# A fifth tile by quarters in both feed-forwards, and the second one's weight sums made in DRAM by accumulating DMAs

## The chip, the cores and the metric

One Trainium2 chip; the kernel runs on one of its cores. The metric is the device time of one execution in microseconds (us), the median of several runs. The engines are named as the profile names them: PE is TensorE (matmuls), with PEld its weight loads; DVE is VectorE, ACT is ScalarE, POOL is GpSimd, and SP is SyncE, which here only issues DMAs. Each engine works through its own queue in order and waits on semaphores for the others.

## The reference

One decoder layer for 512 tokens of width 1024, all in float32:

```python
# x: (1, 512, 1024); D_FF = 2816
x = x + 0.5 * rms_norm(swiglu_ffn(rms_norm(x, pre[0]), ffn1_w_in, ffn1_w_out), post[0])
x = x + rms_norm(token_mixer(rms_norm(x, pre[1]), w_mix_in, ..., w_mix_out), post[1])
x = x + 0.5 * rms_norm(swiglu_ffn(rms_norm(x, pre[2]), ffn2_w_in, ffn2_w_out), post[2])

def swiglu_ffn(x, w_in, w_out):
    gate, up = jnp.split(x @ w_in, 2, axis=-1)
    return (jax.nn.silu(gate) * up) @ w_out
```

The token mixer (two recurrences over chunks, HGRN2 and mLSTM, between two projections) isn't touched by the change.

## The kernel before

The three parts of the layer follow one another: first feed-forward ("f1", about the first 340 us), mixer (to about 600 us), second feed-forward ("f2", to the end).

**Exact products.** Every float32 operand is split into a high part, rounded by ACT (a cast, line 273 for weights, 812 for activations), and a low part, the rest, by DVE (lines 275 and 813). A product takes three matmuls: high by high, high by low, low by high.

**Seven products for eight.** Both feed-forwards multiply by Winograd's form of Strassen's method: two-by-two blocks are multiplied with seven products instead of eight, at the price of sums of blocks before and after. In the first half of a feed-forward (`ffn_in`) the products are called p1 to p7, and each tile `t` of the 11 tiles of 256 hidden columns goes through all seven, 24 matmuls each. Four blocks of raw weights (a, b, c, d) are loaded for a tile, and they are added to one another in place (line 289), by POOL for the early tiles (t under 3) and by DVE for the later ones.

**The output stage** (`ffn_out`) multiplies the gated activations, in 11 tiles k2 of 256 hidden rows, by the output weights. It makes the 1024 output columns in two halves of 512; `OUT` gives the order of the tiles in each half. A tile is done plainly (`plain`, line 893: 48 matmuls of 256 columns) or, if it is in `QUARTERED` for this half, by quarters (`quartered`, line 901: 42 matmuls in seven products). A tile by quarters needs of the activations three quarters (`h_quarters`) and four sums (`h_sums`, then `s_tile`), which are kept if the tile is quartered in both halves; and of the weights three quarters (one item, cut to 768 columns) and four sums, a second item without a load of its own. The sums of weight quarters are made in place in the raw buffer:

```python
for out, a, c in ((1, 1, 0), (0, 0, 2), (2, 1, 2), (3, 2, 3)):
    self.nc.vector.tensor_tensor(b[out], b[a], b[c], op=ALU.add)   # line 306
```

The common part of all quartered tiles of a half is gathered in four PSUM banks M, turned into T at the end (`common`) and added to the output banks C (`add`). The last four tiles (`LAST`) of the second half are held together and done token chunk by token chunk, so that each chunk's norm and residual can follow while PE does the next.

**Buffers.** Four split weights (`w`) are made ahead of PE. Raw weights lie in two rings, `raw` with 3 buffers and `raw2` with 5. Activation tiles of the output stage have a ring `s` of 3; some are put into the dead transposed input instead (`PLACES`, `LATER`, through `x_place`). The quarters of tiles 3 and 7 lie in the ring `raw` ("once"). Tiles 9 and 10 are used in both halves and keep their split (`AGAIN`).

**Order.** The code is traced into one program; a scheduler of the framework then orders each engine's queue by readiness in its own plan, with the order of the code as priority, and assigns buffers and semaphores. Where the code says `behind(...)`, an instruction is queued after another one. `Item` stands for one split weight, `Load` for one DMA; `weights` works out after which item each load is due. Loads go through SP's queue.

Of the kernel before, what the change touches and what calls it, by code (L numbers as in the profile page):

```python
# [8 lines left out]
F32 = mybir.dt.float32  # L9
F32R = mybir.dt.float32r  # L10
AF = mybir.ActivationFunctionType
ALU = mybir.AluOpType
PSUM = bass.MemoryType.PSUM

P = 128
T = 512
D = 1024
# [5 lines left out]
RAW, WBUF, PAD, LATE, NEXT, FRONT, STEP = 3, 4, 128, 112, 64, 96, 16  # L23
# [55 lines left out]

QUARTERED = [(2, 3, 4, 6, 7, 8), (2, 4, 6, 8)]
OUT = [list(range(PAIRS)), [9, 2, 4, 10, 6, 8, 0, 1, 3, 5, 7]]
LAST = 4
PLACES, LATER = {2: 1, 4: 2, 6: 0, 8: 3}, {0: (1, 0), 7: (2, 3)}

AGAIN, ROWS = (9, 10), (18, 19, 20, 21)

# [9 lines left out]
class Load:  # L98


    def __init__(self, key, src, a, b, ring="raw", depth=3, ahead=3, group=None):
        self.key, self.src, self.a, self.b, self.ring, self.depth, self.ahead = key, src, a, b, ring, depth, ahead
        self.group = group


class Item:
# [1 line left out]

    def __init__(self, key, loads, rows=None, adds=(), dst=None, sums=False):
        self.key, self.loads, self.rows, self.adds, self.dst, self.sums = key, loads, rows, adds, dst, sums
        self.reads = {key, *(k for pair in adds for k in pair)}


class Layer:
    def __init__(self, ctx, tc, aps):
        self.tc, self.nc = tc, tc.nc
        self.__dict__.update(aps)
        nc = self.nc  # L120
        pool = lambda name, **kw: ctx.enter_context(tc.tile_pool(name=name, bufs=1, **kw))
        self.cp, self.wp, self.sp, self.psp = pool("cp"), pool("wp"), pool("sp"), pool("psp", space=PSUM)
        self.uid, self.hold = 0, ()
        self.wt, self.free, self.slot = None, deque(), {}

        self.ident = self.cp.tile([P, P], F32, name="ident")
        make_identity(nc, self.ident)
        self.nhalf = self.cp.tile([P, 8], F32, name="nhalf")
        nc.gpsimd.memset(self.nhalf, -0.5)
        self.xs = self.cp.tile([P, NT, D], F32, name="xs")  # L130

        xq = {n: self.cp.tile([P, 2 * D + 2 * STEP * (n == 0)], F32R, name=f"xq{n}") for n in (1, 2, 3, 0)}
        self.xt = [xq[n] for n in range(4)]
        self.xq = [t[:, : 2 * D].rearrange("p (b k t) -> p b k t", b=2, k=KH) for t in self.xt]

        x0 = self.xt[0].rearrange("p (b x) -> p b x", b=2)[:, :, :D].rearrange("p b (k t) -> p b k t", k=KH)
        self.xh = [x0, *self.xq[1:]]
        self.prm = self.cp.tile([P, 36], F32, name="prm")

    def nm(self, s):  # L140
        self.uid += 1
# [108 lines left out]
    def split(self):  # L250

        nc = self.nc
        it = self.items.popleft()
        raw = self.raw[it.key]
        _, a, b = raw.shape
        if it.dst:
            w = it.dst()
        else:
            if self.wt is None:
                self.wt = self.wp.tile([P, 2 * D * WBUF + FRONT + PAD], F32R, name="w")  # L260
            if not self.slot and it.key[0] != "mix":
                self.free = deque(FREE2 if it.key[0] == "f2" else FREE)
            n, o = self.lie("out" if it.key[1] == "out" else "mix" if it.key[0] == "mix" and b == 512 else "any")
            self.free.remove(n)
            w = self.wt[:, o : o + 2 * D].rearrange("p (b k t) -> p b k t", b=2, k=a)
            self.slot[id(w)] = n, o, w
        hi, lo = self.both(w)
        if it.sums:
            raw, hi, lo = (self.flat(v)[:, QUARTER:] for v in (raw, hi, lo))
        self.ready.append((w, it.dst is not None))  # L270
        rows = it.rows
        if rows is None:
            nc.scalar.copy(hi, raw)  # L273
            yield
            self.low = nc.vector.tensor_tensor(lo, raw, hi.bitcast(F32), op=ALU.subtract)  # L275
        else:
            for j in range(a):
                nc.scalar.activation(hi[:, j], raw[:, j], AF.Copy, scale=rows[:, j : j + 1])
            yield
            for j in range(a):  # L280
                nc.vector.scalar_tensor_tensor(  # L281
                    lo[:, j], raw[:, j], rows[:, j : j + 1], hi[:, j].bitcast(F32), op0=ALU.mult, op1=ALU.subtract
                )
        with self.behind(*self.hold):
            for out, other in it.adds:
                o, c = self.raw[out], self.raw[other]

                late = out[1] >= (HEAD if out[0] == "f1" else 1)
                (nc.vector if late else nc.gpsimd).tensor_tensor(o, o, c, op=ALU.add)  # L289
        if it.sums:  # L290
            self.sum_quarters(self.quarters(self.raw[it.key]))
        self.load_due(self.done)
        self.done += 1
        yield
# [487 lines left out]

    def ffn_in(self):

        for p, t in ORDER2[len(HEADS2) :] if self.second else ORDER[len(HEADS) :]:
            with self.behind(*(self.c22 if p == "p3" and self.second else ())):
                self.feed()
            self.c22 = []
            self.lag()
            self.prod(p, t)  # L790
            self.after(p, t)
            if t == PAIRS - 1 and p in ("p3", "p7"):
                self.hs.append(self.h_tile(len(self.hs)))
        self.feed()
        self.lag()
# [26 lines left out]
    def h_quarters(self, k2, n=None):  # L822

        src = self.by_chunk(k2)
        parts = self.x_place(n) if n is not None else [
            self.wp.tile([P, D], F32R, tag="raw", bufs=RAW, name=self.nm("once"))[:, P - 2 * STEP :] for _ in range(2)
        ]
        parts = [v[:, : 3 * QUARTER].rearrange("p (k c t) -> p k c t", c=2, t=P) for v in parts]
        self.two_parts(*(v[:, 0] for v in parts), src[:, 0, 1])
        self.two_parts(*(v[:, 1:] for v in parts), src[:, 1])  # L830
        return [[None] + [v[:, j] for j in range(3)] for v in parts]
# [5 lines left out]
    def h_sums(self, k2, stay):  # L837

        a = self.by_chunk(k2)
        f = self.hf[:, 2 * k2 : 2 * k2 + 2, :]  # L840
        if not stay:
            f = self.sp.tile([P, 2, T], F32, tag="xn", bufs=1, name=self.nm("hsum"))
        v = f.rearrange("p k (c u t) -> p k u c t", u=2, t=P)
        tt = lambda out, x, y, op: self.nc.vector.tensor_tensor(out, x, y, op=op)
        tt(v[:, 0, 0], a[:, 0, 1], a[:, 0, 0], ALU.subtract)
        tt(v[:, 1, 0], v[:, 0, 0], a[:, 1, 0], ALU.add)
        for k in range(2):
            tt(v[:, k, 1], a[:, k, 1], v[:, 1, 0], ALU.subtract)
        return f

    def s_tile(self, f):

        parts = self.s_place()
        self.two_parts(*parts, f)
        parts = [t.rearrange("p k (c u t) -> p k u c t", u=2, t=P) for t in parts]
        return [[t[:, j // 2, j % 2] for j in range(4)] for t in parts]

    def ffn_out(self, gpost_row, scale, after, trans, head):

# [46 lines left out]
        def quartered(C, M, a, s, begin):  # L906

            quarter = lambda t, j: [self.quarters(t[:, b])[j] for b in range(2)]
            A, S = (lambda j: [a[0][j], a[1][j]]), (lambda j: [s[0][j], s[1][j]])
            w = self.pull()  # L910
            product(M["p1"], A(1), quarter(w, 1), begin)
            product(C[1][1], A(3), quarter(w, 3), False)
            product(C[1][0], S(3), quarter(w, 2), False)
            self.drop(w)
            v = self.pull()
            product(M["p7"], S(0), quarter(v, 0), begin)
            product(M["p5"], S(1), quarter(v, 1), begin)
            product(M["p6"], S(2), quarter(v, 2), begin)
            product(C[0][1], A(2), quarter(v, 3), False)
            self.drop(v)  # L920

        def common(M, t):
# [152 lines left out]
    def ffn_items(self, name, w_in, w_out):  # L1075
# [47 lines left out]
        for h in range(2):  # L1123
            for k2 in OUT[h]:
                src = w_out[k2 * 2 * P : (k2 + 1) * 2 * P, h * 512 : (h + 1) * 512].rearrange("(k p) d -> p k d", p=P)
                key = (name, "out", h, k2)
                made.append(Item(key, [Load(key, src, 2, 512, "raw2", 5, 8)], sums=k2 in QUARTERED[h]))
                if k2 in QUARTERED[h]:
                    made.append(Item(key, ()))
                if h == k2 == 0:  # L1130
                    made.append(Item((name, PAIRS - 1, "a"), ()))
# [697 lines left out]
```

## Time and profile before

| | |
|---|---|
| median of 3 runs | 936.55 us (936.34 to 937.08) |
| the profiled execution | 936.35 us, its span 934.6 us |
| granted PE clock | 0.998 of full |
| PE busy | 926.2 us (99%), 7471 matmuls |
| DVE busy | 772.1 us (83%) |
| ACT busy | 511.4 us (55%) |
| POOL busy | 106.5 us (11%) |
| DMA | 101.35 MB, mean 108 GB/s |

The span runs from the first to the last instruction; the rest of the execution's time lies around it. Matmuls overlap, so their mean durations (276 ns) add up to far more than the time between their starts. In the rows of the timeline a start is given first, then a duration, both in us; in those by stretches each engine's busy time comes with its number of instructions, then the granted clock, the share of DMA time and the GB/s.

### The profile page before, as it was taken

What the parts mean: (1) busy time and instruction counts of PE and PEld (TensorE: products, weight loads), DVE (VectorE), ACT (ScalarE), POOL (GpSimd) and SP (SyncE); (2) the same over time, 40 slices, a digit from 0 to 9 for tenths busy, and PEclk for the clock granted to TensorE, in tenths of its full rate; (3) what the DMA queues carried; (4) which work ended last, traced back from release to release, by engine and by line L of the source; (5) the groups of instructions that cost most, each with busy time, mean ns of one, the idle gap of its engine ahead of it and who ended that gap; (6) DMA issues with size and microseconds to landing.
All of it is one profiled execution on the core that took longest, in us unless ns stands there. A gap on an engine that the chain in (4) does not pass through costs nothing.

```text
span 934.6 us, 18052 instructions
## 1 busy us (share of the span) xinstructions
PE 926.2 (99%) x7471; PEld 891.8 (95%) x7471; DVE 772.1 (83%) x1044; ACT 511.4 (55%) x735; POOL 106.5 (11%) x172
## 2 busy tenths in 40 slices
PE   9999999999999999999999999999999999999997
PEld 7999999999999999998887887899999999999997
DVE  6899988889988877698766565799899889998884
ACT  7645454557456466956533445595454545655541
POOL 3530000000001045200010310313000000000101
PEclk9999999999999999999999999999999999999999
DMA  9253343332352025421212124352354435334212
GB/s 313 94 157 91 119 132 113 93 112 71 114 177 91 24 72 134 114 70 54 81 46 69 46 91 150 98 181 70 112 158 136 136 116 159 111 91 126 79 46 91
DMA packets 86956, 101.35 MB, mean 108 GB/s; under 512 B 4277, under 2 KB 66777, under 8 KB 86874
## 3 DMA queue, kind: packets, MB, share of 16 engines
q1 hardware_dynamic: 86586, 99.68, 34.9%
q8 instruction: 58, 0.95, 0.4%
q10 hardware_dynamic: 288, 0.52, 0.2%
q14 instruction: 24, 0.20, 0.1%
HBM read 98.10 MB, written 2.10 MB: 107 GB/s over the span
## 4 chain that ended last, share of the span: by engine, by line
PE 62%; ACT 1%; issue 0%; DVE 0%; POOL 0%; DVEq 0%; POOLq 0%; ACTq 0%
PE ps L603 22%; PE ps L893 7%; PE ps L533 6%; PE ps L901 5%; PE ps L179 5%; PE ps L181 5%; PE ps L180 5%; PE ps L1307 2%; PE ps L348 1%; PE ps L543 1%; PE ps L1488 0%; PE ps L1399 0%; PE ps L1600 0%; PE ps L1573 0%; PE ps L1353 0%; PE ps L1597 0%
## 5 line engine op out<-in xcount | busy, mean ns | idle before, releaser
L273 ACT CAST w<-raw 128x1024 fp32r<-128x1024 f32 (+1 forms) x238 | 244.4, 1035 | 231.7 <-PE ps L603 92.8
L275 DVE TENSOR_TENSOR w<-raw,w 128x1024 fp32r<-128x1024 f32 (+1 forms) x238 | 290.9, 1229 | 38.0 <-ACT w L273 37.5
L603 PE MATMUL ps<-xq,w 128*128 128x256 f32 x2016 | 237.1, 277 | 0.0
L603 PEld LDWEIGHTS ps<-xq,w 128*128 128x128 f32 x2016 | 232.9, 188 | 0.0
L603 PE MATMUL ps<-sq,w 128*128 128x256 f32 x1512 | 178.0, 276 | 0.3
L603 PEld LDWEIGHTS ps<-sq,w 128*128 128x128 f32 x1512 | 174.3, 188 | 1.1 <-ACT ps L654 0.9
L893 PE MATMUL ps<-w,hs 128*128 128x256 f32 x960 | 113.0, 276 | 0.0
L893 PEld LDWEIGHTS ps<-w,hs 128*128 128x128 f32 x960 | 110.7, 188 | 0.0
L289 DVE TENSOR_TENSOR raw<-raw,raw 128x1024 f32<-128x1024 f32 x72 | 89.8, 1251 | 8.3 <-DMA raw<-in_ffn_w_in_dram 6.7
L179 PE MATMUL ps<-w,xq 128*128 128x512 f32 x192 | 78.0, 407 | 0.1
L180 PE MATMUL ps<-w,xq 128*128 128x512 f32 x192 | 74.9, 391 | 0.0
L181 PE MATMUL ps<-w,xq 128*128 128x512 f32 x192 | 74.9, 392 | 0.0
L438 POOL TENSOR_SCALAR col<-col 128x1 f32<-128x1 f32 x24 | 8.3, 347 | 513.4 <-ACT junk L437 513.3
L901 PE MATMUL ps<-w,hs 128*128 128x256 f32 x480 | 57.7, 276 | 0.0
L901 PEld LDWEIGHTS ps<-w,hs 128*128 128x128 f32 x480 | 55.9, 188 | 0.0
L533 PE MATMUL ps<-xq,w 128*128 128x256 f32 x480 | 55.7, 278 | 0.0
L533 PEld LDWEIGHTS ps<-xq,w 128*128 128x128 f32 x480 | 54.9, 188 | 0.5 <-issue 0.5
L179 PEld LDWEIGHTS ps<-w,xq 128*128 128x128 f32 x192 | 36.1, 188 | 8.5 <-issue 0.9
L181 PEld LDWEIGHTS ps<-w,xq 128*128 128x128 f32 x192 | 36.0, 188 | 8.0 <-DVE xq L355 0.3
L812 ACT CAST hs<-hf 128x1024 fp32r<-128x1024 f32 x32 | 33.7, 1052 | 17.5 <-PE ps L901 10.8
L180 PEld LDWEIGHTS ps<-w,xq 128*128 128x128 f32 x192 | 36.1, 188 | 7.3 <-DVE w L281 0.3
L813 DVE TENSOR_TENSOR hs<-hf,hs 128x1024 fp32r<-128x1024 f32 x32 | 39.0, 1217 | 1.3 <-ACT hs L812 1.2
(259 smaller groups left out, 1136.8 us busy)
## 6 DMA issues: line engine op xcount, KB each, us to landing
raw<-in_ffn_w_in_dram SPq DMA_DIRECT2D x98, 512.0 KB, 3.7
raw<-in_ffn_w_out_dram SPq DMA_DIRECT2D x44, 512.0 KB, 4.3
raw<-in_w_mix_in_dram SPq DMA_DIRECT2D x28, 512.0 KB, 3.7
raw<-in_w_mix_out_dram SPq DMA_DIRECT2D x8, 512.0 KB, 3.9
out_dram<-xs SPq DMA_DIRECT2D x8, 256.0 KB, 2.0
xs<-in_x_dram SPq DMA_DIRECT2D x6, 256.0 KB, 4.5
gpost<-in_norm_post_dram SPq DMA_DIRECT2D x3, 512.0 KB, 3.6
gpre<-in_norm_pre_dram SPq DMA_DIRECT2D x2, 512.0 KB, 4.8
```

Of the source, the lines that this page charges most:

```text
L179: mm(ps, sh, mh, start=start, stop=False, **kw)
L180: mm(ps, sh, ml, start=False, stop=False, **kw)
L181: mm(ps, sl, mh, start=False, stop=stop, **kw)
L273: nc.scalar.copy(hi, raw)
L275: self.low = nc.vector.tensor_tensor(lo, raw, hi.bitcast(F32), op=ALU.subtract)
L289: (nc.vector if late else nc.gpsimd).tensor_tensor(o, o, c, op=ALU.add)
L533: mm(ps[:, u0:u1], w[:, a, k, :], self.xop(k, b, u0, u1), start=k + n + m == 0, stop=k == ND - 1 and n == 2, skip_group_check=True,)
L603: self.nc.tensor.matmul(ps[:, c], wb[b][:, k, v], left[d][:, k, :], start=first and a + n + k == 0, stop=n == 2 and k == KH - 1, skip_grou ...
L812: self.nc.scalar.copy(hi, src)
L813: self.nc.vector.tensor_tensor(lo, src, hi.bitcast(F32), op=ALU.subtract)
L893: mm(out, a[kk][:, i * P : (i + 1) * P], w[:, b, kk, QUARTER * v : QUARTER * (v + 1)], start=begin and c == kk == n == 0, stop=kk == 1 and ...
L901: mm(ps[:, QUARTER * c : QUARTER * (c + 1)], A[a][:, c], B[b], start=begin and c == n == 0, stop=n == 2, skip_group_check=True,)
```

## The change

In both feed-forwards tile 3 is done by quarters in the second output half too, and the order of that half changes from 9, 2, 4, 10, 6, 8, 0, 1, 3, 5, 7 to 9, 2, 4, 3, 6, 8, 10, 0, 1, 7, 5. Tile 0's activations go to the ring `s` rather than to the dead input. Tile 3's activation quarters stay in the ring `raw` until its second use, and one of the two parts of tile 7's moves to the buffer of the gain `gpre`. Two of the four sums of activation quarters become one operation.

For the second feed-forward the sums of weight quarters are no longer made by DVE. Eleven tiles in DRAM (one for each half and quartered tile, four slots of 128 x 256) are filled while `ffn_in` of the first feed-forward runs: one copy on SP's queue puts the first quarter into all four slots, and three accumulating DMAs on POOL's queue add the second, third and fourth quarter to the slots that need them. In the code the first of these stands at the products p5 and p3 from tile 3 on, one step further for each tile in the making. In the second feed-forward the sums' item then has a load of its own, from DRAM, and takes its quarters from other slots (`at`).

```diff
-QUARTERED = [(2, 3, 4, 6, 7, 8), (2, 4, 6, 8)]
-OUT = [list(range(PAIRS)), [9, 2, 4, 10, 6, 8, 0, 1, 3, 5, 7]]
-LAST = 4
-PLACES, LATER = {2: 1, 4: 2, 6: 0, 8: 3}, {0: (1, 0), 7: (2, 3)}
+QUARTERED = [(2, 3, 4, 6, 7, 8), (2, 3, 4, 6, 8)]
+OUT = [list(range(PAIRS)), [9, 2, 4, 3, 6, 8, 10, 0, 1, 7, 5]]
+LAST, APART = 4, 7
+PLACES, LATER = {2: 1, 4: 2, 6: 0, 8: 3}, {7: (2, 3)}
...
+        dram = ctx.enter_context(tc.tile_pool(name="sums", bufs=1, space=bass.MemoryType.DRAM))
+        tile_of = lambda h, k2: dram.tile([P, 4, QUARTER], F32, name=f"sums{h}_{k2}")
+        self.sums_of = {(h, k2): tile_of(h, k2) for h in range(2) for k2 in QUARTERED[h]}
...
-        if it.sums:
+        if it.sums == 1:
             self.sum_quarters(self.quarters(self.raw[it.key]))
...
     def ffn_in(self):
 
+        ahead = deque(hk for hk in self.sums_of if not self.second)
+        making = []
         for p, t in ORDER2[len(HEADS2) :] if self.second else ORDER[len(HEADS) :]:
+            if p in ("p5", "p3") and t > FILLED - 2:
+                if ahead:
+                    making.append(self.sums_ahead(*ahead.popleft(), self.ffn2_w_out[0]))
+                making = [g for g in making if next(g, self) is not self]
...
-        parts = self.x_place(n) if n is not None else [
-            self.wp.tile([P, D], F32R, tag="raw", bufs=RAW, name=self.nm("once"))[:, P - 2 * STEP :] for _ in range(2)
-        ]
+        once = lambda pool, tag, bufs, o: pool.tile([P, D], F32R, tag=tag, bufs=bufs, name=self.nm("once"))[:, o:]
+        if n is not None:
+            parts = self.x_place(n)
+        else:
+            places = [(self.wp, "raw", RAW, P - 2 * STEP), (self.cp, "gpre", 1, STEP // 2)]
+            parts = [once(*places[k2 == APART and m]) for m in range(2)]
...
-        for k in range(2):
-            tt(v[:, k, 1], a[:, k, 1], v[:, 1, 0], ALU.subtract)
+        tt(v[:, :, 1], a[:, :, 1], v[:, 1:2, 0].broadcast_to([P, 2, 2, P]), ALU.subtract)
         return f
...
+    def sums_ahead(self, h, k2, w):
+
+        rows = w[k2 * 2 * P : (k2 + 1) * 2 * P, h * 512 : (h + 1) * 512]
+        q = [rows[kk * P : (kk + 1) * P, c * QUARTER : (c + 1) * QUARTER] for kk in range(2) for c in range(2)]
+        to, spread = self.sums_of[h, k2], lambda v, n: v[:, None, :].broadcast_to([P, n, QUARTER])
+        self.nc.sync.dma_start(to, spread(q[0], 4))
+        yield
+        for a, b, v in ((1, 4, q[1]), (0, 3, q[2]), (2, 3, q[3])):
+            self.nc.gpsimd.dma_start(to[:, a:b], spread(v, b - a), accum_op=ALU.add)
+            yield
...
-            v = self.pull()
-            product(M["p7"], S(0), quarter(v, 0), begin)
-            product(M["p5"], S(1), quarter(v, 1), begin)
-            product(M["p6"], S(2), quarter(v, 2), begin)
-            product(C[0][1], A(2), quarter(v, 3), False)
+            v, at = self.pull(), (0, 3, 1, 2) if self.second else range(4)
+            product(M["p7"], S(0), quarter(v, at[0]), begin)
+            product(M["p5"], S(1), quarter(v, at[1]), begin)
+            product(M["p6"], S(2), quarter(v, at[2]), begin)
+            product(C[0][1], A(2), quarter(v, at[3]), False)
...
-                made.append(Item(key, [Load(key, src, 2, 512, "raw2", 5, 8)], sums=k2 in QUARTERED[h]))
-                if k2 in QUARTERED[h]:
+                four = k2 in QUARTERED[h]
+                made.append(Item(key, [Load(key, src, 2, 512, "raw2", 5, 8)], sums=four * (1 + second)))
+                if four and second:
+                    key, src = (*key, "sums"), self.sums_of[h, k2].rearrange("p (a j) f -> p a (j f)", a=2)
+                    made.append(Item(key, [Load(key, src, 2, 512, "raw2", 5, 8)]))
+                elif four:
                     made.append(Item(key, ()))
```

More of the change, by code (lines that the diff above doesn't have):

```diff
@@ L106, with __init__ @@
 class Item:
-    def __init__(self, key, loads, rows=None, adds=(), dst=None, sums=False):
+    def __init__(self, key, loads, rows=None, adds=(), dst=None, sums=0):
         self.key, self.loads, self.rows, self.adds, self.dst, self.sums = key, loads, rows, adds, dst, sums
```

## The prediction

> **What bounds the kernel now.** I read the page's busy times first, then the busy times by stretches of 50 us.
>
> ```profile
> span 934.6 us, 18052 instructions
> PE 926.2 (99%) x7471; PEld 891.8 (95%) x7471; DVE 772.1 (83%) x1044; ACT 511.4 (55%) x735; POOL 106.5 (11%) x172
> ```
> ```profile
> 0.00:50.00 50.00, 48.27 (x368) 44.87 (x369) 37.18 (x48) 32.91 (x57) 21.13 (x29) 1.00 0.58 191
> 50.00:100.00 50.00, 50.00 (x443) 50.00 (x442) 49.66 (x57) 26.12 (x30) 6.14 (x3) 1.00 0.42 129
> ...
> 300.00:350.00 50.00, 49.82 (x436) 49.42 (x435) 40.09 (x56) 27.05 (x54) 12.51 (x24) 1.00 0.18 54
> ...
> 500.00:550.00 50.00, 49.94 (x266) 42.67 (x266) 31.53 (x91) 20.09 (x35) 10.87 (x20) 1.00 0.17 55
> 550.00:600.00 50.00, 49.91 (x242) 40.87 (x241) 29.31 (x43) 24.43 (x52) 6.86 (x18) 1.00 0.44 138
> ...
> 650.00:700.00 50.00, 49.91 (x439) 49.71 (x438) 46.69 (x51) 23.67 (x28) 0.00 (x0) 1.00 0.47 148
> ...
> 750.00:800.00 50.00, 49.76 (x433) 49.20 (x433) 45.88 (x51) 25.53 (x33) 0.00 (x0) 1.00 0.45 138
> 800.00:850.00 50.00, 50.00 (x444) 50.00 (x443) 47.35 (x75) 30.40 (x39) 0.00 (x0) 1.00 0.31 95
> 850.00:900.00 50.00, 50.00 (x444) 50.00 (x443) 43.54 (x62) 29.85 (x44) 2.44 (x8) 1.00 0.34 106
> 900.00:934.60 34.60, 28.59 (x253) 28.39 (x251) 19.77 (x30) 6.85 (x19) 4.60 (x12) 0.96 0.17 61
> ```
> TensorE (PE) is busy 926.2 of 934.6 us. Of the 8.4 us that it is not, 1.73 lie in the first stretch and 6.01 in the last, behind the last matmul; between them the rows add up to 0.18 + 0.06 + 0.09 + 0.09 + 0.24 = 0.66 us. So time is won only by matmuls that fall away, and it is lost by anything that makes PE wait. VectorE (DVE) matters only where it is nearly full as well: 49.66 of 50 us in 50:100.
>
> **Part 1: a fifth tile by quarters in the second output half, in both feed-forwards.** PE's timeline prices a tile:
>
> ```profile
> 297.48 5.60 PE L893 MATMUL ps<-w,hs 128*128 128x256 f32 x48
> 302.92 1.52 PE L901 MATMUL ps<-w,xq 128*128 128x256 f32 x12
> ...
> 312.44 5.60 PE L893 MATMUL ps<-w,xq 128*128 128x256 f32 x48
> 317.88 4.24 PE L893 MATMUL ps<-w,hs 128*128 128x256 f32 x36
> ```
> The plain tile 10 (line 893, 48 matmuls) runs from 297.48 to 302.92, 5.44 us. Tiles 6 and 8 by quarters (line 901, 42 matmuls each) fill 302.92 to 312.44, 4.76 us each. Tile 3 goes from the one kind to the other: 0.68 us less, in each of two feed-forwards: **-1.36 us**. Matmuls come every 113 ns, not the 276 ns that one lasts, since they overlap.
>
> What it costs DVE, in the first feed-forward:
>
> ```profile
> 298.43 2.09 DVE L275 TENSOR_TENSOR w<-raw,w 128x1024 fp32r<-128x1024 f32 x2 [1.17 <-ACT w L273]
> 300.44 1.22 DVE L813 TENSOR_TENSOR hs<-hf,hs 128x1024 fp32r<-128x1024 f32 x1
> 301.58 1.80 DVE L306 TENSOR_TENSOR raw<-raw 128x256 f32<-128x256 f32 x4
> 304.57 1.23 DVE L275 TENSOR_TENSOR w<-raw,w 128x1024 fp32r<-128x1024 f32 x1 [1.19 <-ACT w L273]
> ```
> A tile by quarters asks of DVE the low part of three weight quarters (2.09 - 1.23 = 0.86), the four sums (1.80), the low part of the sums (1.23) and that of the activation sums (1.22): 5.1 us, against PE's 4.76. Tiles 2, 4, 3, 6 and 8 now stand in a row; tile 10, which asks DVE for one weight and relieved it between 4 and 6, comes after them. The cover is what is ready ahead: four weight buffers. Tile 8's second weight is ready at 304.57 + 1.23 = 305.8. Its use begins three products after 307.68 (302.92 + 4.76), 18 matmuls, at 309.7, so 3.9 us ahead. Three more tiles in a row lose 3 x 0.34 = 1.0 us of it. If DVE also waits for ScalarE (ACT), 1.19 us a tile in the last row, they lose 4.6 and PE stalls 0.7. So 0 to 0.7 us; I take **+0.2**, nearer to zero, because the activation sums can fill that wait.
>
> The end of the output stage is tighter. The last four tiles were 1, 3, 5, 7; they become 0, 1, 7, 5, with tile 10 just before them, and tile 10 holds a weight buffer and one of three activation buffers until its last matmul.
>
> ```profile
> 318.08 1.05 ACT L273 CAST w<-raw 128x1024 fp32r<-128x1024 f32 x1 [4.06 <-PE ps L893]
> ```
> ```profile
> 318.33 1.28 DVE L863 TENSOR_TENSOR ps<-ps,hf 128x512 f32<-128x512 f32 x2
> 319.52 1.21 DVE L275 TENSOR_TENSOR w<-raw,w 128x1024 fp32r<-128x1024 f32 x1
> ```
> Before, only the last weight waited for such a release (PE done at 317.88, cast at 318.08, low part done at 320.73). It is first used 3 x 12 matmuls after 317.88, at 321.96: 1.2 us to spare. After, the fourth tile's activations wait for the same release, so one more low part (1.22, L813 above) ends last: about 0.0 us to spare, between -0.4 and +0.5 depending on DVE's order. I take +0.2 in each feed-forward, **+0.4**.
>
> The remaining edits of this part lie off the path. In the sums of activations two DVE operations become one. The quarters of tile 7 that go to the gain's buffer are needed long after the gain was used. Tile 3 keeps two of the three raw buffers until its second use, so two of the mixer's first weights load later; the mixer starts at about 342 and tile 3 ends some 40 us earlier, while a load takes 3.7 us (below). If that cover were gone, PE would wait for those 3.7 us.
>
> **Part 2: the second feed-forward's weight sums from DRAM.** It removes 40 DVE operations:
>
> ```profile
> L306 DVE TENSOR_TENSOR raw<-raw 128x256 f32<-128x256 f32 x40 | 16.8, 421 | 0.8
> ```
> That is 16.8 us of DVE time in a stage where PE never waits (50.00 of 50 in both stretches, 800 to 900), so **0** on the path. It adds 11 loads of 512 KB to that stage's 22.
>
> ```profile
> raw<-in_ffn_w_in_dram SPq DMA_DIRECT2D x98, 512.0 KB, 3.7
> raw<-in_ffn_w_out_dram SPq DMA_DIRECT2D x44, 512.0 KB, 4.3
> ```
> ```profile
> 50.00:225.00 175.00, 175.00 (x1543) 175.00 (x1542) 159.93 (x175) 97.19 (x122) 6.14 (x3) 1.00 0.37 115
> ```
> At a share of 0.37 the DMA engines move 115 GB/s, so about 311 GB/s when full: 1.7 us for 512 KB. A quartered tile then asks 3.4 us of them in 4.76. A load is issued about five weights before its use, 5 x 2.38 = 11.9 us, and takes 4.3. I take **0**; without that cover each of the 11 loads could show 4.3 - 2.4 = 1.9 us.
>
> In the first feed-forward it adds, for each of 11 tiles, one copy (512 KB) on SyncE's (SP's) queue and three accumulating DMAs (384 + 384 + 128 = 896 KB) on GpSimd's (POOL's), each of which waits for the one before. No row shows an accumulating DMA. At the copy rate, copies and sums take 11 x (1.7 + 2.95) = 51 us of full DMA time; if each accumulation also reads its destination at that rate, 11 x (1.7 + 5.9) = 84 us. I take the lower for the likeliest case, as every row that I have is a plain transfer. [...] Either fits the 175 us of this stage beside the 0.37 x 175 = 65 us of weights: 116 to 149 of 175. So **0** on the path if the sums are spread over the stage, as the code spreads them.
>
> **Sum:** -1.36 + 0.2 + 0.4 = -0.76 us. The profiled execution took 936.35 us (934.6 of span), 0.2 less than the median of 936.55. I forecast **935.8** on the median's scale. About 0.2% (1.9 us) is what a measurement can tell from no change, so this is no change.
>
> **Rivals.**
>
> *A. Slower: the sums run early and hold up POOL's own work.* In the code the sums stand from the fourth tile on, but the order of a queue is not that of the code:
>
> ```profile
> 27.13 0.36 SPq L152 DMA_DIRECT2D gpost<-in_norm_post_dram  x1
> 28.28 0.36 SPq L152 DMA_DIRECT2D gpre<-in_norm_pre_dram  x1
> 54.96 3.83 SPq L236 DMA_DIRECT2D raw<-in_ffn_w_in_dram  x3
> ```
> ```profile
> 40.82 2.40 POOL L289 TENSOR_TENSOR raw<-raw,raw 128x1024 f32<-128x1024 f32 x1 [6.15 <-DVE w L275]
> 47.92 2.40 POOL L289 TENSOR_TENSOR raw<-raw,raw 128x1024 f32<-128x1024 f32 x1 [4.69 <-DVE w L275]
> 51.48 5.82 POOL L289 TENSOR_TENSOR raw<-raw,raw 128x1024 f32<-128x1024 f32 x2 [1.16 <-DVE col L1149]
> 282.06 0.19 POOL L438 TENSOR_SCALAR col<-col 128x1 f32<-128x1 f32 x1 [224.75 <-ACT junk L437]
> ```
> ```profile
> 50.35 1.06 ACT L273 CAST w<-raw 128x1024 fp32r<-128x1024 f32 x1 [2.61 <-POOL raw L289]
> ...
> 57.33 1.05 ACT L273 CAST w<-raw 128x1024 fp32r<-128x1024 f32 x1 [0.16 <-POOL raw L289]
> ```
> The gains of the output stage, used after 280, were loaded at 27 and 28: a transfer that waits for nothing is pulled into the first hole of its queue, and SP has one from 28 to 55. The copies wait for nothing, and the accumulations only for them. POOL works in order; if accumulations stand ahead of its additions at 47.92 and 51.48, these wait for DMAs, ACT for them (2.61 us already now), and PE behind. Price: with half of the accumulations ahead of the last additions, POOL gets there at 28 + 18.7 (copies) + 16 to 32 = 63 to 79, 11 to 27 late. The four weights ahead cover at most 4 x 2.72 = 11 us, and with DVE full I take half, 5. PE loses 6 to 22: 942 to 957. It decides from the point where an accumulation that is still moving stands ahead of 51.48. Against it: POOL is free from 57 to 282, and the code begins the sums there.
>
> *B. Slower: DMA becomes the bound in the first feed-forward.* With the sums at the upper price and spread as written, two tiles' sums fall on one tile of products (7 x 24 matmuls, 19.05 us): 2 x 7.6 + 4 x 1.7 = 22.0 us of DMA in 19.05. Over 5.5 tiles PE falls 16 us behind, less some 10 that loads run ahead: +6, 941. It decides from a price of two moves on.
>
> *C. Slower: POOL's DMA issues hold DVE.*
>
> ```profile
> 39.52 1.22 DVE L275 TENSOR_TENSOR w<-raw,w 128x1024 fp32r<-128x1024 f32 x1
> ...
> 41.70 2.61 DVE L275 TENSOR_TENSOR w<-raw,w 128x1024 fp32r<-128x1024 f32 x1 [0.36 <-ACT w L273]
> ```
> Beside POOL's addition of 40.82 the same operation took 2.61 us, not 1.22. If each of 33 issues cost 1.39 us so, DVE would lose 46 us in a stage where it has 175 - 159.93 = 15 left: 31 us, 966. [...]
>
> *D. Faster by over 0.2%:* the waits that I add don't come and all 0.66 us of inner gaps close: -2.0, 934.5.
>
> **How the numbers follow.** Hidden as forecast 0.49 (its own range 935.2 to 936.7: -1.36 with no wait, or with 0.7 + 2 x 0.4 of waits), A 0.28, B 0.10, C 0.05, D 0.08. Faster 0.08, same 0.49, slower 0.43. The range 934.6 to 948 leaves out half of D (0.04), C (0.05) and the upper part of A (some 0.11).
>
> **What would show it.** Right: 12 matmuls less, the quartered tiles still 4.76 us apart, no L306 after 800, and PE 50.00 in 50:100. Wrong: copies on SP before 55 us and a wait of POOL's L289, or of ACT for it, longer than now (A); DVE or ACT waiting for the DMA of raw weights between 70 and 225 (B); L275 above 1.3 us beside POOL's issues (C); a PE gap before the last tile of either output stage, which would mean that I took its cover too long.

## The result, and the profile after

The changed kernel takes 982.74 us (median of 5 runs, 980.76 to 985.5) against 936.55 for the kernel before, beside which it ran: 1.0489 times as long, 95% interval 1.0469 to 1.051. It is 46 us slower where no measurable change was forecast. The profiled execution has a span of 979.0 us, 44.4 more than before.

The page's busy times, the rows of PE and of the granted clock over 40 slices (24.5 us each; 9 is 90% or more), and the queue of the accumulating DMAs (packets, MB, share of the time of 16 DMA engines):

```profile
span 979.0 us, 18084 instructions
PE 931.7 (95%) x7459; PEld 895.8 (91%) x7459; DVE 763.4 (78%) x998; ACT 511.5 (52%) x737; POOL 140.5 (14%) x205
PE   9923999999999999999999999999999999999997
PEclk9975999999999999999999999999999999999999
q0 software_dynamic: 10384, 10.09, 7.2%
```
PE has 12 matmuls fewer, as forecast, and its busy time still grew by 5.5 us. DVE does 46 operations less. So PE's idle time grew by 38.9 us, and PE's row shows where: the third and fourth slice, where the clock falls too. The busy times by stretches (columns: PE, PEld, DVE, ACT, POOL, granted clock, DMA share, GB/s):

```profile
50.00:75.00 25.00, 5.85 (x50) 5.61 (x49) 2.07 (x5) 0.00 (x0) 10.38 (x10) 0.70 1.02 188
75.00:100.00 25.00, 10.54 (x73) 10.54 (x74) 11.76 (x13) 8.22 (x11) 18.77 (x14) 0.61 1.00 134
```
Before, PE was busy 50.00 of 50 us in 50:100, and DVE 49.66. Now everything stands but POOL and the DMA engines. The timelines of SP, POOL, ACT and PE say why; the bracket is the idle time ahead of the row and what ended it.

```profile
26.87 24.63 SPq L874 DMA_DIRECT2D sums<-in_ffn_w_out_dram  x11
...
96.44 13.65 SPq L239 DMA_DIRECT2D raw<-in_ffn_w_in_dram  x7
```
```profile
24.00 4.88 POOL L292 TENSOR_TENSOR raw<-raw,raw 128x1024 f32<-128x1024 f32 x2 [2.66 <-DVE w L278]
...
36.70 2.92 POOL L292 TENSOR_TENSOR raw<-raw,raw 128x1024 f32<-128x1024 f32 x1
...
39.85 3.42 POOL L292 TENSOR_TENSOR raw<-raw,raw 128x1024 f32<-128x1024 f32 x1
...
61.83 2.12 POOL L877 DMA_DIRECT2D sums<-in_ffn_w_out_dram  x2 [6.92 <-DMA sums<-in_ffn_w_out_dram]
...
73.78 2.81 POOL L292 TENSOR_TENSOR raw<-raw,raw 128x1024 f32<-128x1024 f32 x1
...
84.67 3.66 POOL L292 TENSOR_TENSOR raw<-raw,raw 128x1024 f32<-128x1024 f32 x1
...
93.55 5.22 POOL L292 TENSOR_TENSOR raw<-raw,raw 128x1024 f32<-128x1024 f32 x2
```
```profile
76.62 1.04 ACT L276 CAST w<-raw 128x1024 fp32r<-128x1024 f32 x1 [27.36 <-POOL raw L292]
88.36 1.04 ACT L276 CAST w<-raw 128x1024 fp32r<-128x1024 f32 x1 [10.70 <-POOL raw L292]
```
```profile
50.12 5.73 PE L606 MATMUL ps<-xq,w 128*128 128x256 f32 x48
89.46 10.81 PE L606 MATMUL ps<-sq,w 128*128 128x256 f32 x73 [33.61 <-ACT w L276]
```
All eleven copies stand in SP's first hole, from 26.87 on. The accumulations follow them into POOL's queue, ahead of POOL's own additions (line 292, line 289 before). There are eight of these additions in both kernels; before, the first four stood here:

```profile
23.74 4.87 POOL L289 TENSOR_TENSOR raw<-raw,raw 128x1024 f32<-128x1024 f32 x2 [2.66 <-DVE w L275]
29.78 4.89 POOL L289 TENSOR_TENSOR raw<-raw,raw 128x1024 f32<-128x1024 f32 x2 [1.16 <-DVE w L275]
```
The fifth, which ran at 40.82 before, now runs at 73.78, and the sixth at 84.67 instead of 47.92, behind accumulations that wait again and again for the DMA ahead of them. ACT waits 27.36 us for the fifth, then 10.70 for the sixth, and PE, which needs the weight behind the sixth, stands for 33.61 us. SP's next weight load is issued at 96.44 instead of 54.96. This is rival A.

### The profile page after: what moved, and what is told of

The parts are those of the page before. It is cut to its first block, busy times and chain, and to the rows that moved or that the text cites. A ratio compares the mean times of both kernels' runs of the same rounds, so it can differ in the third digit from the quotient of the medians.

```text
span 979.0 us, 18084 instructions
## 1 busy us (share of the span) xinstructions
PE 931.7 (95%) x7459; PEld 895.8 (91%) x7459; DVE 763.4 (78%) x998; ACT 511.5 (52%) x737; POOL 140.5 (14%) x205
## 3 DMA queue, kind: packets, MB, share of 16 engines
q1 hardware_dynamic: 93978, 111.22, 37.7%
q0 software_dynamic: 10384, 10.09, 7.2%
HBM read 119.72 MB, written 17.96 MB: 141 GB/s over the span
## 4 chain that ended last, share of the span: by engine, by line
PE 61%; DVE 3%; issue 1%; ACT 1%; POOL 0%; DVEq 0%; POOLq 0%; ACTq 0%
PE ps L606 21%; PE ps L915 8%; PE ps L536 6%; PE ps L923 5%; PE ps L182 5%; PE ps L184 5%; PE ps L183 4%; PE ps L1333 2%; DVE w L278 1%; PE ps L351 1%; DVE hs L822 1%; PE ps L546 1%; DVE raw L309 1%; PE ps L1514 0%; PE ps L1425 0%
## 5 line engine op out<-in xcount | busy, mean ns | idle before, releaser
L278 DVE TENSOR_TENSOR w<-raw,w 128x1024 fp32r<-128x1024 f32 (+1 forms) x240 | 293.4, 1227 | 79.3 <-ACT w L276 78.6
L606 PE MATMUL ps<-sq,w 128*128 128x256 f32 x1512 | 181.0, 279 | 36.0 <-ACT w L276 33.6
L606 PEld LDWEIGHTS ps<-sq,w 128*128 128x128 f32 x1512 | 176.9, 190 | 37.3 <-ACT w L276 33.8
L915 PE MATMUL ps<-w,hs 128*128 128x256 f32 x960 | 114.0, 277 | 0.1
L915 PEld LDWEIGHTS ps<-w,hs 128*128 128x128 f32 x960 | 111.3, 188 | 0.3 <-DVE w L278 0.3
L923 PE MATMUL ps<-w,hs 128*128 128x256 f32 x528 | 64.3, 277 | 0.7 <-DVE w L278 0.7
L923 PEld LDWEIGHTS ps<-w,hs 128*128 128x128 f32 x528 | 61.8, 188 | 1.3 <-DVE w L278 1.3
L822 DVE TENSOR_TENSOR hs<-hf,hs 128x1024 fp32r<-128x1024 f32 x36 | 43.9, 1220 | 9.7 <-ACT hs L821 9.7
L821 ACT CAST hs<-hf 128x1024 fp32r<-128x1024 f32 x36 | 37.8, 1051 | 25.2 <-PE ps L923 11.6
L877 POOL DMA_DIRECT2D sums<-in_ffn_w_out_dram x33 | 39.5, 1333 | 62.3 <-DMA sums<-in_ffn_w_out_dram 62.1
L182 PEld LDWEIGHTS ps<-w,xq 128*128 128x128 f32 x192 | 36.1, 188 | 8.5 <-issue 0.8
L184 PEld LDWEIGHTS ps<-w,xq 128*128 128x128 f32 x192 | 36.0, 188 | 8.1 <-DVE xq L358 0.3
```

Of the source, the lines that this page charges most:

```text
L182: mm(ps, sh, mh, start=start, stop=False, **kw)
L184: mm(ps, sl, mh, start=False, stop=stop, **kw)
L606: self.nc.tensor.matmul(ps[:, c], wb[b][:, k, v], left[d][:, k, :], start=first and a + n + k == 0, stop=n == 2 and k == KH - 1, skip_grou ...
L822: self.nc.vector.tensor_tensor(lo, src, hi.bitcast(F32), op=ALU.subtract)
L877: self.nc.gpsimd.dma_start(to[:, a:b], spread(v, b - a), accum_op=ALU.add)
L915: mm(out, a[kk][:, i * P : (i + 1) * P], w[:, b, kk, QUARTER * v : QUARTER * (v + 1)], start=begin and c == kk == n == 0, stop=kk == 1 and ...
```

## The experiments

Q: the loss is the order of POOL's queue (A). D: the sums crowd out weight loads on the DMA engines (B). P: the fifth tile itself costs more than it saves, since DVE can't follow. "Ratio" is the time against before on the same chip, with its 95% interval.

**The copies behind the weight loads (e1_paced).**
```diff
-        self.nc.sync.dma_start(to, spread(q[0], 4))
+        with self.behind(self.loaded):
+            self.nc.sync.dma_start(to, spread(q[0], 4))
```


> The change, but each copy into DRAM is queued on SP behind the last weight load traced so far, so that copies and accumulations are spread over the first feed-forward. Theory Q (the 46 us are POOL's additions of raw weights stuck behind accumulations in POOL's in-order queue): no wait of ACT for POOL's L292 beyond the 2.6 us of before, 935 to 937 us. Theory D (the accumulations fill the DMA engines, weights land late): 22 to 25 us of DMA work fall on 19.05 us of products, DVE and ACT wait for raw weights, 941 to 955 us.

939.53 us, ratio 1.0034 (1.0022 to 1.0046): 43 of the 46 us are gone with one line. That is above Q's 935 to 937 and under D's 941 to 955. In the edit, `self.loaded` is the latest weight load in the code. The first copy now stands at 64.58, POOL's additions are back where they were, and the first accumulation comes after them:

```profile
47.79 2.40 POOL L292 TENSOR_TENSOR raw<-raw,raw 128x1024 f32<-128x1024 f32 x1 [4.69 <-DVE w L278]
51.35 5.82 POOL L292 TENSOR_TENSOR raw<-raw,raw 128x1024 f32<-128x1024 f32 x2 [1.16 <-DVE col L1176]
72.33 1.52 POOL L878 DMA_DIRECT2D sums<-in_ffn_w_out_dram  x1 [15.16 <-DMA sums<-in_ffn_w_out_dram]
```
Three things remain: a wait where the sums are dense (ACT's row and PE's),

```profile
161.68 1.04 ACT L276 CAST w<-raw 128x1024 fp32r<-128x1024 f32 x1 [4.25 <-DMA raw<-in_ffn_w_in_dram]
163.27 5.72 PE L606 MATMUL ps<-sq,w 128*128 128x256 f32 x48 [1.74 <-ACT ps L657]
```
a wait for DVE in the first output stage, and slower matmuls later in that stage (both below).

**Only POOL's order mended, the copies still early (e3_pool_behind).**
```diff
-            self.nc.gpsimd.dma_start(to[:, a:b], spread(v, b - a), accum_op=ALU.add)
+            with self.behind(self.pool_add):
+                self.nc.gpsimd.dma_start(to[:, a:b], spread(v, b - a), accum_op=ALU.add)
```


> The change, copies early on SP as in it, but the accumulations are queued on POOL behind POOL's additions (but for one, which the last addition follows). Theory Q: the wait of 33.6 us goes, at most some 5 us are left for the one accumulation ahead, 936 to 942 us. Theory D: the accumulations now meet the seven weight loads of 55 to 66 us, which land late; DVE waits for raw weights by 10 us or more, 945 to 960 us.

943.96 us, ratio 1.0082 (1.0067 to 1.0097). `self.pool_add` is POOL's latest addition. The 33.61 us wait is gone with the copies still at 28.03, so it was POOL's order. The time lies between Q's 936 to 942 and D's 945 to 960: some 4 us are left over the run before. The rows point to crowding: with a DMA share of 1.12 in 60:110 (0.90 in e1_paced), DVE waits for a weight's load and PE for DVE.

```profile
97.06 1.23 DVE L292 TENSOR_TENSOR raw<-raw,raw 128x1024 f32<-128x1024 f32 x1 [3.27 <-DMA raw<-in_ffn_w_in_dram]
99.48 8.36 PE L608 MATMUL ps<-xq,w 128*128 128x256 f32 x56 [2.40 <-DVE w L278]
```
And the granted clock fell behind this wait (third column from the right):

```profile
100.00:102.00 2.00, 2.00 (x14) 2.00 (x14) 2.00 (x3) 1.21 (x2) 0.64 (x1) 0.63 1.10 192
102.00:104.00 2.00, 2.00 (x11) 2.00 (x11) 2.00 (x4) 1.27 (x2) 1.31 (x2) 0.51 1.16 214
```
That is about 3.4 us at half the clock, so some 1.7 us more. PE's gaps over the whole span are 2.1 us longer than in e1_paced. The profiled execution, the slowest of four, is 7.4 us above that of e1_paced, so about half of that stays open.

**Plain writes in place of the accumulations (e4_plain_writes).** The sums are left out: the second feed-forward gets the last quarter that was written.
```diff
-            self.nc.gpsimd.dma_start(to[:, a:b], spread(v, b - a), accum_op=ALU.add)
+            self.nc.gpsimd.dma_start(to[:, a:b], spread(v, b - a))
```


> The change with the three accumulating DMAs of each tile as plain writes of the same bytes on POOL's queue in the same order (leaves out the accumulation). Under Q the additions still stand behind them, but if a plain write takes half the DMA time of an accumulation, the queue moves about twice as fast after the copies: 33.6 us of wait become 12 to 22, 955 to 968 us. If an accumulation costs no more DMA time than a plain write, it stays at 975 to 985 us. The DMA time per 1 KB packet of POOL's queue (109 ns in the change) shows which.

968.2 us, ratio 1.0331 (1.0318 to 1.0345); PE's wait shrinks from 33.61 to 21.98 us. The same bytes took

```profile
q0 software_dynamic: 2992, 10.09, 3.9%
```
3.9% of 966.8 us, 37.7 us of full DMA time, against 7.2% of 979.0, 70.5 us, with the addition: 1.9 times as much. The two also differ in their packets, 2992 (2464 of 4 KB) against 10384 (9856 of 1 KB). Beside packets of the same size the factor is about the same: in the changed kernel's trace a 1 KB packet of POOL's queue takes 113.5 ns in the mean, a plain one (weights on their way to the core) 54.7. The price sets how long POOL is held, not whether.

**The fifth tile alone, in both feed-forwards, in the first, in the second; all sums by DVE (e2_quarters_alone, e10_f1_quarters, e7_f2_quarters).**
```diff
-                made.append(Item(key, [Load(key, src, 2, 512, "raw2", 5, 8)], sums=four * (1 + second)))
-                if four and second:
+                made.append(Item(key, [Load(key, src, 2, 512, "raw2", 5, 8)], sums=four * 1))
+                if False:
...
+PLANS = [
+    ([(2, 3, 4, 6, 7, 8), (2, 3, 4, 6, 8)], [list(range(PAIRS)), [9, 2, 4, 3, 6, 8, 10, 0, 1, 7, 5]], {7: (2, 3)}, 7),
+    ([(2, 3, 4, 6, 7, 8), (2, 4, 6, 8)], [list(range(PAIRS)), [9, 2, 4, 10, 6, 8, 0, 1, 3, 5, 7]], {0: (1, 0), 7: (2, 3)}, None),
+]
```
The first lines are in all three kernels. `PLANS` has a line for each feed-forward (tiles by quarters, order, places); this one is e10's, and in e7 the two lines are exchanged.

> Part 1 alone: the fifth tile by quarters in both feed-forwards, the sums made by DVE as before. If part 1 costs nothing but what the prediction took: 12 matmuls less, 0.68 us less in each output stage, 0 to 0.7 us of waits in the first and 0 to 0.4 at the end of each: 935.2 to 936.7 us. If DVE can't follow five tiles in a row: a PE wait for DVE's L278 of over 1 us in each output stage, 937 to 940 us.

> The fifth tile by quarters in the first feed-forward alone, all sums by DVE. In both it was 4.6 us above before, in the second alone 2.2 (ratio 1.0023). P: a wait of PE for DVE of some 0.7 to 1 us at the second weight of the fourth quartered tile, matmuls 118 instead of 113 ns apart behind it, 2 us above before, ratio 1.002. If it's the second feed-forward that carries the whole cost: ratio 0.999.

> The fifth tile by quarters in the second feed-forward alone, all sums by DVE. With the fifth tile in both feed-forwards the time was 941.0, 4.6 above before, and PE waits of 0.46, 0.72, 0.31 and 0.43 us stood in the second output stage: 1.9 us. P: 1.9 - 0.68 = 1.2 above before, 937.6, which leaves 3.4 for the first feed-forward. If the first feed-forward carries no cost of its own, this run has the whole 4.6: 941.

In both 940.99 us, ratio 1.0043 (1.003 to 1.0056); first alone 938.99, 1.0019 (1.0011 to 1.0028); second alone 939.9, 1.0023 (1.0012 to 1.0033). Each costs about 2 us, where gains of 0.3 (first) and 0.5 us (second) were forecast. In both together it is a little more than P said (937 to 940), and the waits are shorter than its 1 us. In the first output stage of e2_quarters_alone:

```profile
304.70 0.96 PE L920 MATMUL ps<-w,hs 128*128 128x256 f32 x7
306.38 2.22 PE L920 MATMUL ps<-w,hs 128*128 128x256 f32 x17 [0.72 <-DVE w L275]
...
314.26 8.64 PE L912 MATMUL ps<-w,hs 128*128 128x256 f32 x72
322.74 1.58 PE L912 MATMUL ps<-w,xq 128*128 128x256 f32 x12
```
The wait stands at tile 6, the fourth in the row. The last of the seven matmuls ahead of it started 0.28 us (one matmul) before their end, at 305.38, and the next at 306.38, so it costs 1.00 - 0.11 = 0.89 us. The 72 plain matmuls later take 322.74 - 314.26 = 8.48 us, 117.8 ns each, not 113.3: another 0.32 us in these rows alone, with the granted clock at 1.00. But this pace isn't tied to the wait: in e10_f1_quarters the wait is as long (0.75 us) and the same 72 matmuls come 113.3 ns apart, against what was expected of it. DVE's waits are the same kind in the second feed-forward (0.18, 0.45 and 0.16 us of gaps in e7_f2_quarters).

**Tile 10 between (e11_f1_ten_between).** As e10_f1_quarters, with another order:
```diff
-    ([(2, 3, 4, 6, 7, 8), (2, 3, 4, 6, 8)], [list(range(PAIRS)), [9, 2, 4, 3, 6, 8, 10, 0, 1, 7, 5]], {7: (2, 3)}, 7),
+    ([(2, 3, 4, 6, 7, 8), (2, 3, 4, 6, 8)], [list(range(PAIRS)), [9, 2, 4, 3, 10, 6, 8, 0, 1, 7, 5]], {7: (2, 3)}, 7),
```


> The fifth tile by quarters in the first feed-forward alone, but the plain tile 10 between tiles 3 and 6, where it relieves DVE after three quartered tiles instead of coming after five; the last four tiles stay. P (DVE loses time on each quartered tile, and five in a row use up what is ready ahead): the wait at the fourth quartered tile goes, and with it the slower matmuls behind it: 2 us below the run with five in a row, 0.7 below before. If the wait comes from tile 3 as such (its activations and sums, wherever the plain tile stands): the same as that run.

939.93 us, ratio 1.0039 (1.0027 to 1.0051): no gain. The expected wait did go: nothing stands at the fourth quartered tile. But the matmuls were slow from 269 to 325, and a wait came at the mixer's first product (the first row lies ahead of the moved tile):

```profile
271.89 17.12 PE L916 MATMUL ps<-w,hs 128*128 128x256 f32 x144
...
303.69 5.82 PE L916 MATMUL ps<-w,hs 128*128 128x256 f32 x48
309.34 1.58 PE L924 MATMUL ps<-w,xq 128*128 128x256 f32 x12
...
344.28 4.98 PE L546 MATMUL ps<-xq,w 128*128 128x256 f32 x40 [0.73 <-ACT w L276]
```
The plain tile takes 309.34 - 303.69 = 5.65 us, not 5.44. In e10_f1_quarters the 144 matmuls of the first row ran at the faster pace:

```profile
272.18 16.48 PE L916 MATMUL ps<-w,hs 128*128 128x256 f32 x144
```
So in e11 the slow stretch began over 30 us before tile 10's new place, and between 12 and 344 PE has no gap over 0.1 us. P was right on what causes the wait, and removing it didn't bring the time back here; what the wait alone is worth isn't shown, since the pace changed as well.

**The sums in DRAM alone, and spread thinner (e8_sums_thin, e5_thin, e6_f2_thin).** Half as many sums begun per product; the rest begin in the output stage. The copies stay behind the weight loads, here and in all runs below. e8: ten tiles, old tiles and order. e5: the whole change. e6: both parts in the second feed-forward alone.
```diff
-                if ahead:
+                if ahead and p == "p5":
...
+                ahead, making = self.sums_left
+                if ahead and n % 2:
+                    making.append(self.sums_ahead(*ahead.popleft(), self.ffn2_w_out[0]))
+                making[:] = [g for g in making if next(g, self) is not self]
```
The last four lines stand in the output stage, one step for each tile.

> The sums in DRAM alone (ten tiles, spread as in the run with half as many begun), with the old tiles by quarters and the old order in both feed-forwards. 40 additions of DVE in the second output stage go, where PE didn't wait: no gain, and if the sums are thin enough no cost, 936.4 (within 0.5). D at the price of two moves (75 us of full DMA time were seen for eleven tiles) with any crowding left: 937.5 to 938.

> The paced kernel with half as many sums begun per product of the first stage; those that are left begin in the output stage, one for every second tile. The paced kernel took 939.5 us, with a PE wait of 1.74 us at 161.5, where ACT waited 4.25 us for a weight's load. D (the sums crowd out weight loads where they are dense): that wait goes, 937.8. If the wait is an order of instructions and not crowding: still 939.5. The 0.7 us wait of PE for DVE in the first output stage stays with both, since it belongs to part 1.

> Both parts in the second feed-forward alone, the sums spread as in the run before; the first feed-forward has its old four quartered tiles and old order. P (the fifth tile costs in the first output stage, because DVE can't follow five quartered tiles in a row, and the second stage is free of that once its sums come from DRAM): 0.68 us less than before and no new wait of PE, 935.7. If the sums in DRAM cost time wherever they stand: 937 or more. If the second output stage loses as much as the first: 938.

e8: 937.47 us, ratio 1.0004 (0.9995 to 1.0014). The sums alone, well placed, cost nothing that can be told, and bring nothing. e5: 946.68, 1.0097 (1.0079 to 1.0114); e6: 946.09, 1.0092 (1.0078 to 1.0107). The wait at 161 went in e5, as D says, but a larger one came that no theory had priced. POOL, ACT, DVE and PE in e5:

```profile
294.80 0.85 POOL L878 DMA_DIRECT2D sums<-in_ffn_w_out_dram  x1 [5.44 <-DMA sums<-in_ffn_w_out_dram]
295.41 0.47 POOL L441 TENSOR_SCALAR col<-col 128x1 f32<-128x1 f32 x1
```
```profile
295.92 0.38 ACT L440 ACTIVATE junk<-ps 128x256 f32<-128x256 f32 x1 [7.37 <-POOL col L441]
```
```profile
296.42 0.98 DVE L478 TENSOR_TENSOR y<-ps,gpost 128x256 f32<-128x256 f32 x2 [7.27 <-ACT junk L440]
```
```profile
296.90 2.93 PE L924 MATMUL ps<-w,hs 128*128 128x256 f32 x12 [4.95 <-DVE y L478]
```
A short operation on one column stood behind an accumulation that waited for its DMA, and the wait went through ACT and DVE to PE. It is Q again at another place. Behind it the clock was granted at 0.65, 0.50, 0.50 and 0.64 in the four stretches of 2 us from 294 on, about 6.8 us at half: some 3.4 us more, so that wait and clock make 8.4 of the 9.5 us by which e5 lies above before. In e8 the last accumulation is issued 10 us before that column's operation:

```profile
272.91 0.85 POOL L881 DMA_DIRECT2D sums<-in_ffn_w_out_dram  x1 [6.48 <-DMA sums<-in_ffn_w_out_dram]
282.71 0.19 POOL L444 TENSOR_SCALAR col<-col 128x1 f32<-128x1 f32 x1 [8.94 <-ACT junk L443]
```

**The sums spread evenly over the first stage's sixteen products p5 and p3 (e9_f2_even, e12_even).** e9: both parts in the second feed-forward alone. e12: the whole change.
```diff
-                if ahead:
+                visit += 1
+                if ahead and visit * 11 // 16 > (visit - 1) * 11 // 16:
```


> Both parts in the second feed-forward alone, the first as before, the eleven sums begun evenly over the sixteen products of the first stage, none left for the output stage. In the run with sums left for the output stage, GpSimd waited there for its DMA until 294.80 with the additions for the norm (282.71 in the run of the sums alone) behind it, and PE waited 5.63 us. Q (GpSimd's queue works in order, so whatever stands behind an accumulation waits for its DMA): without a sum there, that wait goes, 940; and as the sums alone cost nothing, 0.68 us less than before for the fifth tile: ratio 0.999. If the wait of 5.63 us came from part 1: still 946.

> The whole change with its copies behind the weight loads and its sums begun evenly over the sixteen products of the first stage. Q and D: no wait of GpSimd in the output stage and none of ACT for a weight at 161, so what is left is part 1 in the first output stage (1.0 us of wait and the slower matmuls behind it, less 0.68), while the second stage gains 0.68 without a wait since DVE has no sums there: ratio 1.001, 938. If the crowding is still there: a PE wait between 60 and 200 with a DMA at its end, 939.5 or more.

e9: 936.73 us, ratio 0.9999 (0.999 to 1.0008). e12: 938.49, 1.0019 (1.001 to 1.0027). Each lies 0.001 above what Q and D said. Once PE has begun, none of its gaps over 0.1 us ends on a DMA or on POOL in either. In e9 the five quartered tiles run without a wait,

```profile
878.43 1.52 PE L929 MATMUL ps<-w,xq 128*128 128x256 f32 x12
...
902.23 8.32 PE L921 MATMUL ps<-w,hs 128*128 128x256 f32 x72
910.39 1.52 PE L921 MATMUL ps<-w,xq 128*128 128x256 f32 x12
```
(902.23 - 878.43) / 5 = 4.76 us each, and the 72 plain matmuls come 113.3 ns apart. Where DVE makes the sums (e7) the second feed-forward costs 0.23%, here nothing: that difference, 2 us, is what the sums in DRAM are worth, and only together with the fifth tile. No kernel that ran is measurably faster than before.

## Why the prediction was wrong

**The failed step** is "0 on the path if the sums are spread over the stage, as the code spreads them". The code's place is not the queue's: nothing held the copies back, so all stood at 26.87. The rows that show this for the gains were quoted under A, and I still gave the code's place the larger chance. The reason I wrote against A, that POOL is free from 57 on and the code begins the sums there, was the error itself. What the runs showed in its place: with the sums at the head of the queue PE waits 33.61 us, and e1_paced, which holds only the copies back, gave back 43 of the 46 us. A was on the list with a chance of 0.28, with the right mechanism and too small a price.

**A's price** (942 to 957) was mis-sized. I held up the additions of 47.92 and 51.48 and had the latter reached at 63 to 79, 11 to 27 late. That of 40.82 was held already, to 73.78; that of 47.92 ran at 84.67, 37 late, and that of 51.48 at 93.55, 42 late. Ahead of these three stood 11, 16 and 19 of the 33 accumulations, where the sum had half of them ahead of the last, at 1 to 2 us of full DMA time each; they took 2.1 in the mean (70.5 / 33). So PE waited 33.61 us and not 6 to 22. And the wait brought slow matmuls with it. The stretches around it (granted clock in the third column from the right):

```profile
50.00:60.00 10.00, 5.85 (x50) 5.61 (x49) 2.07 (x5) 0.00 (x0) 2.91 (x3) 1.00 1.05 201
60.00:70.00 10.00, 0.00 (x0) 0.00 (x0) 0.00 (x0) 0.00 (x0) 2.97 (x3) 0.51 1.09 211
...
92.00:94.00 2.00, 2.00 (x11) 2.00 (x11) 1.93 (x4) 1.99 (x5) 1.23 (x2) 0.50 0.94 91
94.00:96.00 2.00, 2.00 (x18) 2.00 (x18) 2.00 (x1) 0.37 (x1) 2.00 (x2) 0.93 0.97 128
```
The 73 matmuls of 89.46 took 10.81 us against 8.4 at 113.3 ns. The trace has the clock at 0.50 from some 4 us after PE stopped until some 4.8 us after it started again. In e3_pool_behind it fell behind a wait of 2.40 us; behind the 1.74 us of e1_paced it stayed at 1.00 (the stretch 150:200).

**The accumulation's price.** I took the lower bound, 51 us with the copies, "as every row that I have is a plain transfer". In that sum the accumulations are 32 us, in the upper one 65; they alone took 70.5 us, 1.9 times the plain writes of e4. So the upper bound was the nearer one, and still a little low. Whether an accumulation also reads its destination, as that bound supposed, no run shows: the pages count 119.72 MB read from HBM with the addition (the changed kernel) and without it (e4). The price made A longer by 14.5 us (982.74 against 968.2). B alone is real but small, where I had +6: PE waits of 1.74 us in e1_paced and 2.40 in e3, none once the sums were even (e12).

**Part 1.** -1.36 held: 12 matmuls, 4.76 us per quartered tile. The +0.2 for DVE (0 to 0.7) did not: one wait of 0.89 us, smaller ones, and stretches of slower matmuls. The step that failed is that three more tiles lose 1.0 us of a cover of 3.9. That cover had been built by tile 10 itself, on which PE spends 5.44 us and DVE one low part, 1.23 (its activations keep their split), so moving it away takes 4.2 us more: 3.9 - 1.0 - 4.2 = -1.3. This is a reckoning, and it comes near the 0.89 that was measured. e11_f1_ten_between agrees: with tile 10 in between the wait is gone. The last four tiles, +0.2 each (-0.4 to +0.5), were about right: gaps of 0.16 us at 323.43 (e10) and at 912.38 (e7). At the mixer's first weights, which I had left off the path, PE waits 0.45 us for DVE in e10, 0.10 before; what holds DVE there isn't shown. For DVE's sums in the second feed-forward "0" was right without the fifth tile (e8) and 2 us short with it (e7 against e9); I had read the stage as it was before, not as part 1 leaves it. The cover of the loads there held (e12).

Of the 44.4 us between the two profiled executions, PE's gaps give 38.7, the half clock 2.4, the slower pace described at the end 1.4 and the matmuls' tails behind some eight gaps 1.3, less 1.36 for the matmuls that went; some 2 us stay open.

**Rival C** fell: line 278, the operation priced, in e1 between 75 and 192, and the same operation (line 275) before:

```profile
L278 DVE TENSOR_TENSOR w<-raw,w 128x1024 fp32r<-128x1024 f32 x45 | 54.7, 1218 | 5.4 <-ACT w L276 5.3
```
```profile
L275 DVE TENSOR_TENSOR w<-raw,w 128x1024 fp32r<-128x1024 f32 x45 | 54.8, 1219 | 3.1 <-ACT w L273 3.0
```
1218 ns beside 30 issues of POOL, 1219 without: the issues cost this operation nothing in the mean. In the changed kernel one L278 took 4.69 us (at 36.03), but beside POOL's additions of 36.70 and 39.85, which tells nothing of the issues.

## What to carry to other kernels

A DMA that waited for nothing went to the first hole of its queue here, wherever the code had it (the gains at 27.13 and 28.28 before, the copies at 26.87 after): give it something to wait for, or read its place from the queue's order. What works in order, as POOL does here, must have nothing that waits for a DMA ahead of work on the critical path, however small; an operation on one column that stood behind such a wait cost PE 4.95 us (e5). And a cover is to be priced with the plan as it will be: find out which step builds it before moving that step.

## What the runs showed of the hardware

- **Two paces of matmuls at the same granted clock.** 128x256 matmuls come 113.3 or 117.8 ns apart with the clock at 1.00. The pace changed at short interruptions and lasted until another one: in the changed kernel two matmuls start 0.41 us apart at 365.37, and the 104 from 366.12 on come 117.8 ns apart, up to the transposes at 378.49. It did not change at each of them: before, two start 0.36 us apart at 341.40, with 113.3 ns on both sides. In e9 the mixer ran slow from 352 to 408 (117.8 ns in the row of 355.14), behind the same gaps as before, where it ran fast from 353 on (113.3 in that of 355.05): matmul 3000 of the execution starts at 349.67 in both, matmul 3500 at 408.78 in e9 and at 406.94 before. These 1.8 us are more than the fifth tile's 0.68. The profiled execution of e9 (937.92) is 1.2 us above its kernel's median, so the pace may belong to an execution and not to the kernel. What sets the pace was not found: no run isolates it.
- **An accumulating DMA from DRAM to DRAM** took 1.9 times the DMA time of a plain write of the same bytes in larger packets. POOL's issue took 1.3 us in the mean, and a single wait of POOL for the landing of the one before up to 6.9 us in the changed kernel (62.1 us in 20 waits):

```profile
POOL sums L877 <- DMA sums<-in_ffn_w_out_dram: 62.1, 20, 6.9
```
- **Half the clock behind waits of PE.** The granted clock fell to 0.50 for about 34 us around the 33.61 us wait, for about 6.8 behind one of 4.95 (e5) and for about 3.4 behind one of 2.40 (e3).
